# Feed-forward activations of an encoder trunk turned by block turns on VectorE and a trip through device memory instead of transposes on TensorE

## The chip, the cores and the metric

The kernel runs on one core of one Trainium2 chip. The metric is device time in microseconds for one launch. The kernel before was run three times: 1505.3, 1506.34 and 1506.68 us, median 1506.34 us.

## The reference, cut to what matters

Two layers over 512 tokens of width 1024, all in float32. Each layer adds a token mixer (windowed attention in layer 0, gated linear attention in layer 1) and then a feed-forward part:

```
def swiglu(h, w_gate_up, w_down):
    g, u = jnp.split(h @ w_gate_up, 2, axis=-1)
    return (jax.nn.silu(g) * u) @ w_down
...
for i in range(DEPTH):
    ...
    h = h + swiglu(rms_norm(h, ffn_norm[i]), ffn_w_gate_up[i], ffn_w_down[i])
```

`w_gate_up` is 1024 x 5632 (2816 gate and 2816 up columns), `w_down` is 2816 x 1024. The change touches only this part, which runs twice.

## The kernel before, in words

**Layout.** The residual `h` is kept with its 1024 features on partitions (8 tiles of 128 x 512 tokens). Every float32 operand of a large product is split into a high part (a copy on ScalarE, line 96) and a low part (a subtraction on VectorE, line 97), and a product is three matmuls: high by high, high by low, low by high.

**Gate and up** (`gate_up`, line 332). The 2816 hidden columns go in six chunks `j`: five of width 512 and a last one of width 256. The gate/up product of a chunk is done by a scheme with seven block products in place of eight (calls of `product`, lines 317 to 330; 24 matmuls each, results in PSUM banks `pp` and `s`). Here the activations are the stationary operand, so a chunk's result has tokens on partitions: `h1` (tokens 0 to 255) and `h2` (tokens 256 to 511), each 128 partitions x 2 x width, in buffers `g`. ScalarE copies results out of PSUM (line 367), VectorE combines and scales them (lines 381, 409, 410, 419, 431), ScalarE applies SiLU (lines 382, 429). `h1` is complete about when the sixth product runs, `h2` shortly after the seventh ends.

**Weights of a chunk** (`forms`, line 237). Each product needs a sum of blocks of the weight matrix. The sums are made by loads on SyncE's queue (SP, line 246, into `wA`, `wB`, `wf`) and accumulating loads on GpSimd's queue (line 251), and one by VectorE (line 296). The loads of a chunk are issued a chunk ahead; the accumulating loads can start only when the block before was split out of the same buffer. Split tiles `wh` and `wl` have three buffers each, so a split waits until the product three tiles back is through.

**The turn** (`turn`, line 348). The down product needs the activations with hidden columns on partitions. So 22 tiles `acts` of 128 x 512 are made, four per chunk of 512 columns. Before, each is four TensorE transposes of 128 x 128 (line 353) into a PSUM bank `t` or `o`, and one copy by ScalarE (line 355). The four turns of chunk `j` stand between the first five products of chunk `j+1`; the two of the last chunk stand among the first matmuls of the down product.

**Down** (`halves`, `down_part`, `down`, lines 441 to 477). Each of the 22 tiles is split into high and low parts (lines 446, 447). Then for each of the 8 output tiles `m`, 22 x 3 matmuls accumulate in a `pp` bank (`mm3`, lines 108 to 110), and VectorE adds the result to the old `h`, which was parked in device memory (`kept`) and is loaded again (line 473; the add is line 475). Down weights are loaded in three pieces per `m` into two buffers `wf` (line 103) and split. The first two tiles of the down product are started while the last chunk still runs.

**Order.** A scheduler with priorities and explicit "issue after" hints puts the instructions on each engine; each engine, and each DMA queue, then takes its own list strictly in order. An instruction that waits holds everything behind it on the same engine or queue.

Of the kernel before, what the change touches and what calls it, by code (L numbers as in the profile page):

```python
# [13 lines left out]
F32 = mybir.dt.float32  # L14
F32R = mybir.dt.float32r
AF = mybir.ActivationFunctionType
# [5 lines left out]
P = 128  # L22
D = 1024
S = 512
KT = D // P
NT = S // P
# [3 lines left out]
NH = HID // P  # L30
# [9 lines left out]
class Trunk:  # L40
# [291 lines left out]
    def gate_up(self, layer, acts):  # L332
        nc = self.nc
        ACT, DVE = nc.scalar.activation, nc.vector
        weights = [self.forms(self.ins["gate_up"][layer, j], j == 0, 0 if j else 2 * AHEAD) for j in range(5)]
        weights.append(self.forms(self.ins["gate_up_last"][layer], True))
        self.minus = self.t("Rc", (P, 256))
        first = next(weights[0])
        DVE.tensor_scalar(self.minus[:, 0:4], self.cols[:, self.col0 + 4:self.col0 + 8], -1.0, None, op0=ALU.mult)
        S1, S2, S3, S4 = [[(hi[:, i], lo[:, i]) for f, hi, lo in self.sums] for i in range(4)]  # L340
        self.kept = self.dr.tile([KT, P, S], F32, name=f"h_dram_{layer}")
        cut = lambda lo: [tuple(e[:, lo:lo + 256] for e in self.x[m]) for m in range(KT // 2, KT)]
        A11, A12, A22 = self.x[0:KT // 2], cut(0), cut(256)

        done = None
        late = [self.t("xs") for _ in range(NH - KT)]

        def turn(c):
            if done is None:
                return  # L350
            pt = self.p("to"[c % 2])
            for i in range(NT):
                nc.tensor.transpose(pt[:, i * P:(i + 1) * P], done[i // 2][:, i % 2, c * P:(c + 1) * P], self.ident)
            a = self.t("h") if len(acts) < KT else late[len(acts) - KT]
            ACT(a, pt, AF.Copy)
            acts.append(a)

        for j in range(6):
            width = 512 if j < 5 else 256
            w = weights[j]  # L360
            pair = lambda tag: [self.p(tag) for _ in range(2)]
            keep = lambda: self.t("g", (P, 2, S))

            def copy(src):
                out = keep()
# [11 lines left out]
            turn(1)  # L377
            def gates():
                for i in range(2):
                    e = g1[:, i, 0:width]  # L380
                    DVE.tensor_add(e, b2[i][:, 0:width], e)
                    ACT(e, e, AF.Silu, scale=R[:, i:i + 1])

            if j > 0:
                gates()
            b3 = pair("s")
            x5 = next(w)
            if j == 0:
                with self.tc.issue_after(self.low.ins):
                    self.last_sums()  # L390
            self.product(b3, S1, x5, width, True)
            turn(2)
# [7 lines left out]
            turn(3)  # L400
# [12 lines left out]
            if j == 4:  # L413
                before = self.copied
                with self.tc.high_priority(offset=AHEAD), self.tc.issue_after(before.ins):
                    early = [self.split(a, (P, S), tag, tag) for a, tag in zip(acts, ("a", "xs"))]
            for i in range(2):
                e = h2[:, i, 0:width]
                DVE.tensor_add(e, p5[:, i, 0:width], e)
            x4 = next(w)  # L420
            if j == 0:
                with self.tc.issue_after(self.added.ins):
                    for m in range(KT):
                        nc.gpsimd.dma_start(self.kept[m], self.h[m])
            self.product(b1, A22, x4, width, False)
            g2 = keep()
            for i in range(2):
                e = g2[:, i, 0:width]
                silu = ACT(e, b1[i][:, 0:width], AF.Silu, scale=R[:, 2 + i:3 + i])
                u = h2[:, i, 0:width]  # L430
                DVE.scalar_tensor_tensor(u, u, R[:, 6 + i:7 + i], e, op0=ALU.mult, op1=ALU.mult)
# [3 lines left out]
        self.started = self.down_part(self.p("pp"), layer, 0, 0, 2, early)  # L435
        for c in range(2):
            turn(c)
        with self.tc.issue_after(silu.ins):
            nc.scalar.preload_act_table_set("natural_log_exp_and_others")

# [21 lines left out]
    def down(self, layer, acts, col_next):  # L462
        nc = self.nc
        ps, pairs = self.started
        for k in range(len(pairs), NH):
            pairs.append(self.halves(acts[k], k))
        self.x = [None] * KT
        for m in range(KT):
            if m > 0:
                ps = self.p("pp")  # L470
            self.down_part(ps, layer, m, 2 if m == 0 else 0, NH, pairs)
            h = self.t("h")
            nc.sync.dma_start(h, self.kept[m])
# [751 lines left out]
```

## Time and profile before

| what | value |
|---|---|
| median of three runs | 1506.34 us |
| the profiled execution | 1506.73 us |
| its span, first to last instruction | 1504.9 us |
| first feed-forward part: chunks 1 to 4 | 628.6 to 789.7 us, about 40.2 us each |
| chunk 5 and the start of the down product | 789.7 to 829.5 us |
| second feed-forward part: transposes seen from, to | 1198.8 to 1382.8 us |
| granted TensorE clock | 1.000 |

Times are in us from the span's start unless marked ns. PE is TensorE, PEld its weight loads, DVE VectorE, ACT ScalarE, POOL GpSimd, SP SyncE, which issues DMAs. A row of a group says how often an instruction ran, its busy time and the mean of one. Matmuls overlap: each takes about 390 ns from start to end, but the next starts 227 ns later, so steps between starts, not durations, tell what TensorE spends.

### The profile page before, as it was taken

The page shows a single profiled execution, that of the slowest core. Times are in us where ns is not written, and L with a number is a line of the kernel's source. Part 1 is how long each engine was busy: PE and PEld are TensorE (multiplying, and loading weights), DVE is VectorE, ACT ScalarE, POOL GpSimd, SP SyncE. Part 2 cuts the span into 40 slices and gives each one's busy share as a digit, 9 for nine tenths or more (in the row PEclk, how much of TensorE's full clock was granted, in tenths as well). Part 3 has the DMA queues.
Part 4 walks back from the last instruction along what each step waited for, and adds up shares of the span by engine and source line. Part 5 has one row for each costly group of instructions (what it writes and reads, how often), then busy time and mean ns, then how long its engine had stood idle before and what let it go on. Part 6 is the DMA issues. An engine that isn't in the chain of part 4 may idle for free.

```text
span 1504.9 us, 21152 instructions
## 1 busy us (share of the span) xinstructions
PE 1490.5 (99%) x8142; PEld 1226.2 (81%) x8142; DVE 950.4 (63%) x1732; ACT 784.9 (52%) x1352; POOL 110.2 (7%) x192
## 2 busy tenths in 40 slices
PE   8999999999999999999999999999999999999998
PEld 6878788877878878888889887888888888889887
DVE  6584666768477778866667334947576866668222
ACT  6353453545366655755567323546644855568121
POOL 0001010101010011211110000000010211110000
PEclk9999999999999999999999999999999999999999
DMA  7412222243222137776664333212155676675331
GB/s 277 163 60 93 85 82 84 79 125 99 84 71 71 43 111 204 224 166 146 151 152 135 104 91 104 88 57 84 47 160 185 196 172 152 156 151 147 121 107 60
DMA packets 59829, 183.95 MB, mean 122 GB/s; under 512 B 10032, under 2 KB 10608, under 8 KB 59728
## 3 DMA queue, kind: packets, MB, share of 16 engines
q1 hardware_dynamic: 44912, 133.17, 26.6%
q0 software_dynamic: 14816, 49.42, 16.2%
q8 instruction: 64, 1.05, 0.3%
q14 instruction: 37, 0.30, 0.1%
HBM read 174.11 MB, written 8.46 MB: 121 GB/s over the span
## 4 chain that ended last, share of the span: by engine, by line
PE 87%; DVE 8%; ACT 2%; DMA 1%; issue 1%; SPq 0%; ACTq 0%; DVEq 0%
PE ppp L109 9%; PE ppp L108 9%; PE ppp L110 9%; PE ppp L548 7%; PE ppp L549 7%; PE ppp L547 7%; PE ppp L328 6%; PE ppp L330 6%; PE ppp L329 6%; PE ps L330 3%; PE ps L328 3%; PE ps L329 3%; PE po L679 2%; DVE wl L97 2%; PE ps L639 1%; PE ps L729 1%
## 5 line engine op out<-in xcount | busy, mean ns | idle before, releaser
L97 DVE TENSOR_TENSOR wl<-wf,wh 128x1024 fp32r<-128x1024 f32 (+1 forms) x184 | 220.3, 1199 | 229.2 <-ACT wh L96 228.5
L96 ACT ACTIVATE wh<-wf 128x1024 fp32r<-128x1024 f32 (+1 forms) x184 | 191.4, 1041 | 319.9 <-PE ppp L109 192.7
L547 PE MATMUL ppp<-wh,xs 128*128 128x512 f32 (+1 forms) x672 | 256.9, 386 | 5.8 <-ACT wh L96 5.5
L548 PE MATMUL ppp<-wl,xs 128*128 128x512 f32 (+1 forms) x672 | 257.8, 384 | 0.6 <-DVE wl L97 0.3
L549 PE MATMUL ppp<-wh,xs 128*128 128x512 f32 (+1 forms) x672 | 257.6, 383 | 0.0
L547 PEld LDWEIGHTS ppp<-wh,xs 128*128 128x128 f32 x672 | 126.8, 189 | 33.1 <-ACT wh L96 5.5
L548 PEld LDWEIGHTS ppp<-wl,xs 128*128 128x128 f32 x672 | 126.8, 189 | 26.4 <-DVE wl L97 2.7
L549 PEld LDWEIGHTS ppp<-wh,xs 128*128 128x128 f32 x672 | 126.9, 189 | 25.0 <-issue 1.3
L97 DVE TENSOR_TENSOR wl<-wA,wh 128x1024 fp32r<-128x1024 f32 x88 | 107.4, 1221 | 37.9 <-ACT wh L96 37.9
L96 ACT ACTIVATE wh<-wA 128x1024 fp32r<-128x1024 f32 x88 | 93.2, 1059 | 62.0 <-PE ppp L330 45.8
L328 PE MATMUL ppp<-wh,a 128*128 128x512 f32 (+1 forms) x288 | 108.2, 381 | 0.0
L329 PE MATMUL ppp<-wl,a 128*128 128x512 f32 (+1 forms) x288 | 107.4, 373 | 0.0
L330 PE MATMUL ppp<-wh,a 128*128 128x512 f32 (+1 forms) x288 | 107.3, 374 | 0.0
L109 PE MATMUL ppp<-xs,wh 128*128 128x512 f32 x272 | 106.6, 393 | 0.0
L108 PE MATMUL ppp<-xs,wh 128*128 128x512 f32 x272 | 106.3, 392 | 0.0
L110 PE MATMUL ppp<-xs,wl 128*128 128x512 f32 x272 | 105.9, 391 | 0.0
L97 DVE TENSOR_TENSOR wl<-wB,wh 128x1024 fp32r<-128x1024 f32 x38 | 46.5, 1225 | 73.7 <-ACT wh L96 73.7
L627 ACT ACTIVATE sm<-sm,st 128x160 f32<-128x160 f32 (+2 forms) x128 | 56.8, 447 | 40.8 <-DVE st L626 40.7
L328 PE MATMUL ps<-wh,sh 128*128 128x512 f32 (+1 forms) x192 | 73.1, 381 | 0.0
L328 PE MATMUL ppp<-wh,sh 128*128 128x512 f32 (+1 forms) x192 | 72.2, 376 | 0.0
L330 PE MATMUL ppp<-wh,sl 128*128 128x512 f32 (+1 forms) x192 | 71.6, 373 | 0.0
L330 PE MATMUL ps<-wh,sl 128*128 128x512 f32 (+1 forms) x192 | 71.5, 373 | 0.0
(323 smaller groups left out, 2957.3 us busy)
## 6 DMA issues: line engine op xcount, KB each, us to landing
wA<-in_gate_up_dram POOLq DMA_DIRECT2D x52, 512.0 KB, 5.4
wf<-in_down_dram SPq DMA_DIRECT2D x32, 512.0 KB, 3.6
wf<-in_gate_up_dram SPq DMA_DIRECT2D x24, 512.0 KB, 4.5
wf<-in_a_w_v_dram SPq DMA_DIRECT2D x20, 512.0 KB, 3.4
wB<-in_gate_up_dram POOLq DMA_DIRECT2D x20, 512.0 KB, 5.5
wf<-in_a_w_q_dram SPq DMA_DIRECT2D x16, 512.0 KB, 3.3
wf<-in_a_w_qk_dram SPq DMA_DIRECT2D x16, 512.0 KB, 3.2
wB<-in_gate_up_dram SPq DMA_DIRECT2D x16, 512.0 KB, 3.2
```

Source lines behind the costliest of these rows:

```text
L96: nc.scalar.activation(hi, src, AF.Copy)
L97: self.low = nc.vector.tensor_sub(lo, src, hi.bitcast(F32))
L108: mm(out, lhsT=wh, rhs=xh, start=start, stop=False)
L109: mm(out, lhsT=wh, rhs=xl, start=False, stop=False)
L110: self.multiplied = mm(out, lhsT=wl, rhs=xh, start=False, stop=stop)
L328: mm(a, lhsT=xh[:, tok], rhs=wh[:, f], start=start and k == 0, stop=False, skip_group_check=True)
L329: mm(a, lhsT=xh[:, tok], rhs=wl[:, f], start=False, stop=False, skip_group_check=True)
L330: self.multiplied = mm(a, lhsT=xl[:, tok], rhs=wh[:, f], start=False, stop=k == last, skip_group_check=True)
L547: mm(a, lhsT=xh, rhs=wh[:, f], start=k == 0, stop=False)
L548: mm(a, lhsT=xh, rhs=wl[:, f], start=False, stop=False)
L549: self.multiplied = mm(a, lhsT=xl, rhs=wh[:, f], start=False, stop=k == KT - 1)
L627: nc.scalar.activation(sm[:, w], sm[:, w], AF.Exp, bias=n, scale=-1.0, accum_out=l)
```

## The change

It replaces the way in which the finished activations get hidden columns on partitions; the arithmetic stays the same.

- `turn` is now on VectorE: one instruction turns a 128 x 512 piece in blocks of 32 x 32 (line 351 of the kernel after). For each 256 hidden columns of a chunk there is a buffer `y` of 128 x 1024, with room in the pool `g`, filled half from `h1` and half from `h2`. That is four block turns per full chunk, two in the last: 22 per layer, 44 in all.
- `put` stores each `y` to device memory (`turned`) by four DMAs on SP's queue (line 359), one for each group of 32 partitions, in runs of 128 numbers (512 bytes). These four put the 32 x 32 blocks where a full transpose would have them, apart from the order of tokens.
- `get` loads one finished tile of 128 x 512 back (line 365), on SP's queue, at the places where a turn stood before. A fetch waits for the four stores of its `y`.
- The tokens of the turned tiles come in another order (within 512: 4 groups of 32 out of each 128). The down product's result has that order too, and the add to `h` (line 489, before 475) reads and writes with a pattern that undoes it.
- TensorE's 176 transposes and ScalarE's 44 copies out of PSUM are gone.

```
-        def turn(c):
-            if done is None:
-                return
-            pt = self.p("to"[c % 2])
-            for i in range(NT):
-                nc.tensor.transpose(pt[:, i * P:(i + 1) * P], done[i // 2][:, i % 2, c * P:(c + 1) * P], self.ident)
-            a = self.t("h") if len(acts) < KT else late[len(acts) - KT]
-            ACT(a, pt, AF.Copy)
-            acts.append(a)
+        turned = self.dr.tile([NH, 4, 32, 4, P], F32, name=f"turned_{layer}")
+
+        def turn(half, done, ys):
+            for n, y in enumerate(ys):
+                f = slice(n * 256, (n + 1) * 256)
+                DVE.transpose(y.rearrange("p b g j -> p g b j")[:, 2 * half:2 * half + 2],
+                              done[:, :, f].rearrange("p i (b j) -> p i b j", j=32))
+
+        def put(ys):
+            for n, y in enumerate(ys):
+                c = 4 * j + 2 * n
+                to = turned[c:c + 2].rearrange("c b i a e -> a i (c b) e")
+                for r in range(4):
+                    nc.sync.dma_start(to[r], y[32 * r:32 * r + 32].rearrange("i b g j -> i b (g j)"))
+
+        def get():
+            c = len(acts)
+            if c < min(4 * j, NH):
+                a = self.t("h") if c < KT else late[c - KT]
+                nc.sync.dma_start(a, turned[c].rearrange("b i a e -> (b i) (a e)"))
+                acts.append(a)
...
-            with self.tc.issue_after(self.multiplied.ins):
-                turn(0)
+            get()
...
+            ys = [self.t("g", (P, 8, 4, 32)) for _ in range(width // 256)]
+            turn(0, h1, ys)
             self.product(b1, S3, next(w), width, False)
...
-            done = (h1, h2)
+            turn(1, h2, ys)
+            put(ys)
...
-            nc.vector.tensor_add(h, ps, h)
+            order = "p (g a j) -> p a g j"
+            nc.vector.tensor_add(h.rearrange(order, a=4, j=32), ps.rearrange("p (a g j) -> p a g j", a=4, j=32),
+                                 h.rearrange(order, a=4, j=32))
```

Line numbers after the diff are larger by 10 to 15 in the kernel after (418, 419, 430, 442, 460 and 489 there are 409, 410, 419, 431, 447 and 475 before).

Three places show what stands where now.

First, SP's queue in the first feed-forward part, about the end of chunk 1. Before, it holds only weight loads (`wA` and one `wf` for chunk 3, then `wf` and `wB` for chunk 3):

```order
L246 DMA wA_7033<-in_gate_up_dram 128x1024
L246 DMA wA_7035<-in_gate_up_dram 128x1024
L246 DMA wf_7080<-in_gate_up_dram 128x1024
L246 DMA wf_7082<-in_gate_up_dram 128x1024
L246 DMA wB_7130<-in_gate_up_dram 128x1024
```

After, the eight stores of chunk 1 (two buffers `g`, four DMAs each) and its four fetches (into `h`) stand between them:

```order
L246 DMA wA_7036<-in_gate_up_dram 128x1024
L246 DMA wA_7038<-in_gate_up_dram 128x1024
L246 DMA wf_7078<-in_gate_up_dram 128x1024
L359 DMA turned_6095<-g_6645 32x8x128 x4
L359 DMA turned_6095<-g_6646 32x8x128 x4
L365 DMA h_6773<-turned_6095 128x512
L365 DMA h_6816<-turned_6095 128x512
L246 DMA wf_7080<-in_gate_up_dram 128x1024
L365 DMA h_6862<-turned_6095 128x512
L365 DMA h_6901<-turned_6095 128x512
L246 DMA wB_7123<-in_gate_up_dram 128x1024
```

The second `wf` load of chunk 3 and its `wB` loads now stand behind stores that wait for the end of chunk 1, and behind fetches that wait for these stores.

Second, VectorE where chunk 4 goes over into chunk 5 in the first feed-forward part. `wl` are weight splits, `a`, `xs` and `wA` from `h` are halves of finished tiles. Before:

```order
L97 TENSOR_TENSOR wl_7609<-wA_7336,wh_7608 128x1024
L419 TENSOR_TENSOR g_7591<-g_7473,g_7591 128x512
L97 TENSOR_TENSOR wl_7646<-wf_7643,wh_7645 128x1024
L97 TENSOR_TENSOR a_7595<-h_6464,a_7594 128x512
L97 TENSOR_TENSOR xs_7599<-h_6512,xs_7598 128x512
L419 TENSOR_TENSOR g_7591<-g_7473,g_7591 128x512
L447 TENSOR_TENSOR wA_7908<-h_6563,wA_7908 128x512
L447 TENSOR_TENSOR wA_7911<-h_6607,wA_7911 128x512
L97 TENSOR_TENSOR wl_7695<-wf_7692,wh_7694 128x1024
```

After:

```order
L351 STREAM_TRANSPOSE g_7534<-g_7493 128x2x8x32
L97 TENSOR_TENSOR wl_7590<-wA_7333,wh_7589 128x1024
L351 STREAM_TRANSPOSE g_7535<-g_7493 128x2x8x32
L430 TENSOR_TENSOR g_7572<-g_7455,g_7572 128x512
L97 TENSOR_TENSOR wl_7637<-wf_7634,wh_7636 128x1024
L97 TENSOR_TENSOR a_7576<-h_6474,a_7575 128x512
L97 TENSOR_TENSOR xs_7580<-h_6517,xs_7579 128x512
L430 TENSOR_TENSOR g_7572<-g_7455,g_7572 128x512
L460 TENSOR_TENSOR wA_7886<-h_6563,wA_7886 128x512
L460 TENSOR_TENSOR wA_7889<-h_6602,wA_7889 128x512
L97 TENSOR_TENSOR wl_7681<-wf_7678,wh_7680 128x1024
```

Two block turns of `h1` have come in ahead of the split (the last row of each piece) that the second product of chunk 5 waits for.

Third, SP's queue at the start of the down product. Before, the weight pieces follow one another (last of `m` = 0, the three of `m` = 1, the first of `m` = 2):

```order
L103 DMA wf_8042<-in_down_dram 128x768
L103 DMA wf_8076<-in_down_dram 128x1024
L103 DMA wf_8106<-in_down_dram 128x1024
L103 DMA wf_8136<-in_down_dram 128x768
L103 DMA wf_8171<-in_down_dram 128x1024
```

After, the stores of the last chunk and its two fetches (`xs`) stand among them:

```order
L103 DMA wf_8010<-in_down_dram 128x768
L365 DMA xs_6091<-turned_6095 128x512
L365 DMA xs_6092<-turned_6095 128x512
L103 DMA wf_8044<-in_down_dram 128x1024
L486 DMA h_8413<-h_dram_6080 128x512
L486 DMA h_8508<-h_dram_6080 128x512
L359 DMA turned_6095<-g_7813 32x8x128 x4
L103 DMA wf_8074<-in_down_dram 128x1024
L103 DMA wf_8104<-in_down_dram 128x768
L365 DMA xs_6093<-turned_6095 128x512
L365 DMA xs_6094<-turned_6095 128x512
```

The last two fetches, of tiles 20 and 21, stand behind the third weight piece of `m` = 1.

More of the change, by code (lines that the diff above doesn't have):

```diff
@@ L343, in gate_up @@
         A11, A12, A22 = self.x[0:KT // 2], cut(0), cut(256)
-        done = None
         late = [self.t("xs") for _ in range(NH - KT)]
-        def turn(c):
-            if done is None:
-                return
-            pt = self.p("to"[c % 2])
-            for i in range(NT):
-                nc.tensor.transpose(pt[:, i * P:(i + 1) * P], done[i // 2][:, i % 2, c * P:(c + 1) * P], self.ident)
-            a = self.t("h") if len(acts) < KT else late[len(acts) - KT]
-            ACT(a, pt, AF.Copy)
-            acts.append(a)
+        turned = self.dr.tile([NH, 4, 32, 4, P], F32, name=f"turned_{layer}")
[16 more added lines that the diff above has]
+                acts.append(a)
         for j in range(6):
@@ L376, in gate_up @@
             self.product(b2, A12, next(w), width, True)
-            turn(1)
+            get()
             def gates():
@@ L391, in gate_up @@
             self.product(b3, S1, x5, width, True)
-            turn(2)
+            get()
             p5 = copy(b3)
@@ L399, in gate_up @@
             self.product(b1, S2, x6, width, False)
-            turn(3)
+            get()
             if j == 0:
@@ L435, in gate_up @@
         self.started = self.down_part(self.p("pp"), layer, 0, 0, 2, early)
+        j = 6
         for c in range(2):
-            turn(c)
+            get()
         with self.tc.issue_after(silu.ins):
```

## The prediction

> **What bounds the kernel now.** I read the page first, then the busy time by stretches, then TensorE instruction by instruction, then the chain of waits. The page's first part gives the engines:
>
> ```profile
> PE 1490.5 (99%) x8142; PEld 1226.2 (81%) x8142; DVE 950.4 (63%) x1732; ACT 784.9 (52%) x1352; POOL 110.2 (7%) x192
> ```
>
> TensorE looks full, but a busy TensorE may only be one whose matmuls overlap. So the stretches of chunks 2 and 3 and the end of the first feed-forward part (length, then busy time and instructions of PE, PEld, DVE, ACT, POOL, then clock, DMA share, GB/s):
>
> ```profile
> 669.10:709.30 40.20, 40.20 (x185) 32.99 (x184) 25.47 (x27) 23.49 (x31) 5.15 (x6) 1.00 0.69 159
> 709.30:749.50 40.20, 40.20 (x185) 32.98 (x184) 25.48 (x27) 23.51 (x31) 5.16 (x6) 1.00 0.67 155
> 789.70:812.90 23.20, 22.77 (x187) 22.19 (x187) 19.29 (x27) 18.95 (x34) 0.86 (x1) 1.00 0.55 161
> ```
>
> Two chunks take 40.20 us each with the same instruction count, at full clock, while VectorE has some 15 us free in each and ScalarE 17. That is a steady issue rate, not a wait. TensorE's rows in time show the rate (start, duration):
>
> ```profile
> 639.45 0.39 PE L328 MATMUL ppp<-wh,a 128*128 128x512 f32 x1
> 639.68 0.39 PE L329 MATMUL ppp<-wl,a 128*128 128x512 f32 x1
> 639.90 0.39 PE L330 MATMUL ppp<-wh,a 128*128 128x512 f32 x1
> 640.14 0.60 PE L353 MATMUL po<-ident,g 128*128 128x128 f32 x4
> 640.49 0.48 PE L328 MATMUL ps<-wh,sh 128*128 128x512 f32 x1
> 640.80 0.40 PE L329 MATMUL ps<-wl,sh 128*128 128x512 f32 x1
> ```
>
> The step from matmul to matmul is 0.227 us. Across a turn, 639.90 to 640.80 is 0.90 us for two steps, which would be 0.45: a turn of four transposes costs the stream 0.45 us. TensorE bounds the chunks, and the transposes are in its stream.
>
> **What is removed.** The rows of the transposes, both PSUM banks:
>
> ```profile
> L353 PE MATMUL po<-ident,g 128*128 128x128 f32 x88 | 14.9, 272 | 0.0
> L353 PE MATMUL pt<-ident,g 128*128 128x128 f32 x88 | 14.5, 274 | 1.0 <-DVE g L431 1.0
> ```
>
> 176 transposes are 44 turns. At 0.45 us each that is 19.8 us. The chunks say a little more: 40.20 less 7 x 24 = 168 matmuls at 0.227 (38.14) is 2.06 us for four turns, because the scheduler cuts one turn of each chunk in two and the stream is disturbed twice (0.7 for that one). Eight chunks (1 to 4, two layers) give 16.5 us; the remaining 12 turns (four beside chunk 5 and two in the down product, per layer) at 0.45 give 5.4. In chunk 5 TensorE also waits for a turn's input:
>
> ```profile
> 792.88 0.36 PE L328 MATMUL ppp<-wh,a 128*128 128x256 f32 x1
> 793.09 0.28 PE L329 MATMUL ppp<-wl,a 128*128 128x256 f32 x1
> 793.80 0.33 PE L353 MATMUL pt<-ident,g 128*128 128x128 f32 x1 [0.43 <-DVE g L431]
> ```
>
> The wait of 0.43 goes too, once a layer: 0.9. Gross gain 16.5 + 5.4 + 0.9 = 22.8 us. ScalarE's 44 copies (line 355) count nothing: ScalarE is not late in the chunks.
>
> The Trainium skill would size this otherwise: "VectorE: DVE Perf Modes", section "The three transpose paths", gives 390 ns for a TensorE transpose of 128 x 128 (bf16) and 311 ns for VectorE's 32 x 32 blocks, and the section "Rules for kernel authors" prefers TensorE for a full 128 x 128. By its figure 176 transposes would be an estimated 68.6 us. The trace does not agree for transposes within a stream: 0.45 us for four is 0.11 each, so less is to be won.
>
> **What is added on VectorE.** 44 block turns of 128 x 512. Before has block turns of 32 columns only; for 512 columns it has other operations:
>
> ```profile
> L667 DVE STREAM_TRANSPOSE t<-sm 128x32 f32<-128x32 f32 x64 | 9.4, 188 | 7.7 <-ACT sm L627 7.4
> L419 DVE TENSOR_TENSOR g<-g,g 128x512 f32<-128x512 f32 x4 | 2.7, 682 | 0.0
> ```
>
> If a block turn runs one column per cycle like the addition, it takes 0.68 us, of which 0.60 count back to back; if each 32 columns paid the 0.19 of the small one, 16 x 0.19 = 3.0. I take 0.68: most of 0.19 us for 32 columns must be fixed cost. Four in a chunk are 2.7 us against 15 free. They stand in line, though: two before the weight splits of the next chunk. In chunks 1 to 4 each split is ready about a microsecond or more before its matmul, so I cost them at nothing there; uncovered they would be 0.6 us each.
>
> Where chunk 4 goes into chunk 5 that cover is gone. The chain of waits runs there through DMA, ScalarE and VectorE and not through TensorE:
>
> ```profile
> 772.75 5.44 DMA wB<-in_gate_up_dram
> ...
> 788.87 1.18 DVE wA L447 x2
> 790.04 0.03 issue
> 790.07 1.02 DVE wl L97
> ...
> 793.08 0.67 DVE g L431
> ```
>
> The split at 790.07, whole length 1.21, ends at 791.28 and now comes behind two block turns: 792.5. Its matmul ran at 793.09; without the turns since that load (a whole one, 0.45, and most of a cut one, 0.6) it would run at 792.0. TensorE waits about 0.5 us, once a layer: 1.0.
>
> The final add reads and writes in groups of 32 numbers, 16 times. Only the last add of the program lies on the path, so I cost it at nothing; bounds 0 and one more pass over it, 0.7 us.
>
> **What is added on the queues.** Per full chunk: eight stores of 128 KB, four fetches of 256 KB. The nearest rows (KB each, median us to landing) and the cost of issuing on SP:
>
> ```profile
> out_dram<-h SPq DMA_DIRECT2D x8, 256.0 KB, 2.0
> h<-h_dram SPq DMA_DIRECT2D x8, 256.0 KB, 3.2
> h_dram<-h POOLq DMA_DIRECT2D x8, 256.0 KB, 7.5
> L1215 SPq DMA_DIRECT2D out_dram<-h x8: 343/344/344, 1396.5 to 1501.2; - x8
> ```
>
> Twelve issues at 0.34 are 4 us of SP per chunk, plus the wait of the fetches for the stores. What waits behind is the next-but-one chunk's `wf` and `wB`: loaded a chunk ahead, they have some 20 us to spare, so this is hidden. The DMA engines get 2 MB more per chunk; the store goes in 512-byte runs. A short stretch that held only 128 such packets and 16 tiny ones, and the queues of chunk 2:
>
> ```profile
> q1 hardware_dynamic: 144, 0.07, 32.2%
> DMA  8999997920000004999799999596492294475849
> q0 software_dynamic: 875, 3.19, 45.4%
> q1 hardware_dynamic: 864, 3.15, 22.8%
> ```
>
> 32.2% of 0.7 us on 16 engines for 128 packets is 28 ns each; 2048 per chunk are 3.6 us of all engines. The fetch, at q1's 9.2 us for 3.15 MB, is 3.1 us. So the share of 0.69 rises to about 0.86 of a shorter chunk; the slices of 1 us show eight empty ones just where the fetches fall. Hidden, with less to spare.
>
> **The down product's start** has least cover. Tiles 20 and 21 go turn, store, fetch, halves. In before's times: VectorE's last line-431 operation ends at 815.5, the turn at 816.2, stores issued by 817.6 and landed by 819.6. The fetches then stand behind the third weight piece of `m` = 1, the last of these four issues:
>
> ```profile
> 809.24 12.61 SPq L103 DMA_DIRECT2D wf<-in_down_dram  x4
> 820.14 1.14 ACT L446 ACTIVATE g<-xs 128x512 fp32r<-128x512 f32 x2
> 826.94 0.39 PE L108 MATMUL ppp<-g,wh 128*128 128x512 f32 x1
> ```
>
> The issues end at 821.85 (809.24 + 12.61), so the fetches issue at 822, land at 825.2 and 825.5, and the halves, made by ScalarE from 820.14 before, are ready by about 826.6 and 827.3. TensorE wanted tile 20 at 826.94 and, two turns earlier, wants it at 826.0: a wait of about 0.5 us a layer, 1.0.
>
> **The sum**, against the profiled execution's own 1506.73 us (span 1504.9 and 1.8 around it): 1506.7 - 22.8 + 1.0 + 1.0 = 1485.9. The median of the runs lies 0.4 below the profiled one: **1485.5 us**. If only 0.45 per turn goes, 1488.5; if neither wait comes, 1483.5.
>
> **The rivals.**
>
> A. The fetches come later still. A store that lands like `h_dram` (7.5 in place of 2.0) lands at 825.1, the halves are ready near 830, and TensorE waits 3.5 us more a layer: 1485.5 + 7 = 1492.5. For it: that row is a store beside accumulating loads. Against: the down product's start has no accumulating load of its own chunk left. Chance 0.13.
>
> B. VectorE sets the end in the chunk change. At 1.4 us a block turn, the two ahead of the split add 1.5 us, the two behind the next sum another 0.7, and the second split of each chunk's seventh product, with 0.6 to spare, is late by 0.1 eight times: about 2 x 2.2 + 0.8 = 5 us, 1490.5. At 3.0 us a turn, some 15 us. For it: the chain already runs through VectorE there. Against: the fixed cost seen at 32 columns. Chance 0.12.
>
> C. Slower: stores crowd the accumulating loads. The second load for a chunk's third product issues at
>
> ```profile
> 669.43 0.85 POOL L251 DMA_DIRECT2D wA<-in_gate_up_dram  x1 [1.95 <-DVE wl L97]
> DMA to landing us min/median/max: 5.2/5.4/10.7
> ```
>
> Its tile is wanted at 669.1 + 60 x 0.227 + 0.9 = 683.6, less 2.3 for the split: 681.3. Stores start at about 674. With a landing at the slowest seen, 680.1, nothing happens. If the stores hold it 13.5 us beyond a usual landing of 674.9, to 688.4, TensorE waits 7 us in each of eight chunks: 1485.5 + 56 = 1541.5. It decides from a delay of 6.4 us, where a wait begins; above 9.0 us (2.6 x 8 = 20.8, all that the sum gains) the change is slower. Against: the stores' own engine time is 3.6 us. "VectorE: DVE Perf Modes", section "The three transpose paths", of the Trainium skill warns that a plain DMA copy that transposes by strides is 19 times slower than one through the crossbar when the innermost stride is large. By that rule C would be the likely case; here the innermost 128 numbers are in one run, and the 28 ns packet speaks against it. Chance 0.08.
>
> D. The same crowding between these points eats the gain to within 0.2% (3 us, about what a measurement of this kernel can tell from no change). Chance 0.04.
>
> **How the numbers follow.** The forecast keeps 0.63, its own range 1483.5 to 1488.5. Faster by over 0.2%: forecast, A and B, 0.88; same 0.04; slower 0.08. The range takes in A, B's nearer half and, below, a microsecond for splits that gain more: 1482.5 to 1495, leaving out C, D and a part of B.
>
> **What would show it.** Chunks of about 38.1 us with 168 matmuls and steps of 0.227 would show the gain; longer steps at a chunk's third or sixth product, released by a DMA, rival C. Line 351's mean is the block turn. A gap before the matmul of chunk 5's second product, and one before tile 20, of about half a microsecond each, are the two costs. Chunks still near 40 us, or a gap of several us in each, would make the prediction wrong.

## The result, and the profile after

The changed kernel takes 1528.64 us (median of four runs, 1525.56 to 1530.77) against 1506.13 before (four runs): 1.0147 times as long, 95% interval 1.0135 to 1.0159. The prediction was 1485.5 us and faster with a chance of 0.88. It was wrong in sign: 43.1 us lie between forecast and result.

The page of the kernel after, its engines, its DMA totals, its chain and the queue of the accumulating loads (KB each, median us to landing):

```profile
PE 1485.6 (97%) x7966; PEld 1212.6 (80%) x7966; DVE 976.5 (64%) x1776; ACT 765.3 (50%) x1308; POOL 110.2 (7%) x192
...
DMA packets 90103, 207.02 MB, mean 136 GB/s; under 512 B 12145, under 2 KB 35249, under 8 KB 90001
...
PE 67%; issue 18%; DVE 7%; DMA 3%; ACT 3%; POOL 2%; POOLq 0%; SPq 0%; ACTq 0%; DVEq 0%
...
L351 DVE STREAM_TRANSPOSE g<-g 128x512 f32<-128x512 f32 x44 | 30.2, 701 | 0.6
...
wB<-in_gate_up_dram POOLq DMA_DIRECT2D x20, 512.0 KB, 7.2
```

TensorE has lost its 176 transposes and 5 us of busy time, and yet idles 38 us (1523.8 less 1485.6) where it idled 14. The block turn takes 0.70 us, as forecast. The last row is the first hint: before, it read

```profile
wB<-in_gate_up_dram POOLq DMA_DIRECT2D x20, 512.0 KB, 5.5
```

Laid beside each other, matmul by matmul, the two kernels keep a steady distance up to the first feed-forward part (after is 1.3 us ahead there) and again between the two parts. All of the loss falls inside them: 9.9 us in layer 0 and 10.4 in layer 1. By part, both layers together, the two traces differ by 11.8 us in chunk 0, 5.4 in chunks 1 to 4, and 3.1 in chunk 5 and the 66 matmuls of the first down output. Chunks 0 to 5 of layer 0, after, in the busy time by stretches (columns as in the prediction):

```profile
588.05:632.72 44.67, 41.47 (x177) 33.03 (x176) 38.41 (x58) 29.84 (x43) 7.80 (x12) 0.96 0.61 183
632.72:676.68 43.96, 40.62 (x170) 32.45 (x168) 27.67 (x30) 22.03 (x27) 4.25 (x5) 0.96 0.72 179
676.68:717.14 40.46, 38.98 (x170) 31.30 (x168) 27.03 (x31) 21.67 (x27) 4.87 (x6) 1.00 0.81 206
717.14:756.65 39.51, 38.84 (x169) 31.23 (x168) 27.40 (x31) 21.88 (x27) 4.94 (x7) 1.00 0.87 213
756.65:796.51 39.86, 39.05 (x169) 31.24 (x168) 27.60 (x31) 24.39 (x32) 6.57 (x8) 1.00 0.83 198
796.51:823.78 27.27, 23.54 (x177) 21.68 (x176) 23.43 (x34) 17.24 (x31) 0.86 (x1) 1.00 0.72 196
```

Before, chunks 0 and 1 took 39.2 and 40.6 and chunk 5 took 23.1; they now take 44.7, 44.0 and 27.3. Chunks 2 to 4 hardly gain: 39.5 to 40.5 where 38.1 was forecast. Within a chunk the loss has one place. Lengths of the seven products of chunk 2, layer 0, from the starts of TensorE's rows (two later runs, explained below, beside them). A length runs to the first matmul of the next product, so a wait for the sixth product's first weight split counts in the fifth:

| kernel | 1 to 4 | 5 | 6 | 7 |
|---|---|---|---|---|
| before | 5.80, 5.81, 5.91, 5.91 | 5.55 | 5.61 | 5.62 |
| after | 5.44, 5.44, 5.44, 5.44 | 6.32 | 6.77 | 5.61 |
| without transposes (`bare2`) | 5.44, 5.44, 5.44, 5.44 | 5.44 | 6.18 | 5.90 |
| the same without the accumulating load of the sixth (`bare_noadd`) | 5.44, 5.44, 5.44, 5.44 | 5.44 | 5.61 | 5.58 |

The first four products have become 24 x 0.227 us, just as forecast; what they win is given back while TensorE waits for the weight splits of the sixth. Who TensorE waits for, in the stretch of chunks 0 to 5, before and then after:

```profile
PE pt L353 <- DVE g L431: 0.4, 1, 0.4
```

```profile
PE ppp L328 <- ACT wh L96: 5.6, 4, 2.6
PE ppp L329 <- DVE wl L97: 4.3, 7, 0.8
PE ppp L328 <- ACT g L377: 2.3, 2, 2.0
PE ps L328 <- ACT g L377: 0.7, 1, 0.7
```

Weight splits come late now, and in chunk 5 copies out of PSUM (line 377). Two things stand out, and they are told apart below.

**At the end of chunk 0 TensorE's order has turned over.** At 622.92 it waits for a split, when no store has been issued yet:

```profile
622.92 0.88 PE L328 MATMUL ppp<-wh,a 128*128 128x512 f32 x2 [1.15 <-ACT wh L96]
624.18 0.80 PE L329 MATMUL ppp<-wl,a 128*128 128x512 f32 x1 [0.38 <-DVE wl L97]
```

The list of TensorE in the built program says why. Before, the seventh product follows the sixth (`ppp_6095` and `ppp_6096` are chunk 0's banks); after, most of the first product of chunk 1 (banks `ppp_6436`, `ppp_6437`) comes in between:

```
before  L330 MATMUL ppp_6096<-wh_6343,sl_6048 128x512
before  L328 MATMUL ppp_6095<-wh_6376,a_5872 128x512
after   L330 MATMUL ppp_6097<-wh_6348,sl_6048 128x512
after   L328 MATMUL ppp_6436<-wh_6442,a_5890 128x512
```

`wh_6442` has to wait for one of the three split buffers, while the seventh product's splits lie ready. Steps over 0.4 us from 622 to 631 add up to 5.3 us of loss.

**In the later chunks an accumulating load lands late.** The four of chunk 1 in the view of line 251 (issues, then the time to landing), before and after:

```profile
L251 POOL DMA_DIRECT2D wB<-in_gate_up_dram x2: 850/850/850, 648.9 to 652.1; - x2
...
DMA to landing us min/median/max: 5.3/5.4/5.5
```

```profile
L251 POOL DMA_DIRECT2D wB<-in_gate_up_dram x2: 850/850/850, 651.9 to 654.6; - x2
...
DMA to landing us min/median/max: 8.9/9.4/9.6
```

and TensorE at the sixth product of chunk 1, after, with 3.3 us of idle time:

```profile
659.70 0.39 PE L330 MATMUL ps<-wh,sl 128*128 128x512 f32 x1
662.66 0.51 PE L328 MATMUL ppp<-wh,sh 128*128 128x512 f32 x1 [2.58 <-ACT wh L96]
663.92 0.50 PE L329 MATMUL ppp<-wl,sh 128*128 128x512 f32 x1 [0.76 <-DVE wl L97]
```

Chunk 5 waits for a late accumulating load too, by way of ScalarE's queue. Its own load took 7.1 us to landing where it took 5.3 before, and the split that needs it stands ahead of the two copies that TensorE waits for, 2.0 us, at 814.91:

```profile
813.53 1.06 ACT L96 ACTIVATE wh<-wA 128x1024 fp32r<-128x1024 f32 x1 [2.50 <-DMA wA<-in_gate_up_last_dram]
```

### The profile page after: what moved, and what is told of

It reads as the page before. It is cut to its first block, busy times and chain, and to the rows that moved or that the text cites. A ratio compares the mean times of both kernels' runs of the same rounds, so it can differ in the third digit from the quotient of the medians.

```text
span 1523.8 us, 21053 instructions
## 1 busy us (share of the span) xinstructions
PE 1485.6 (97%) x7966; PEld 1212.6 (80%) x7966; DVE 976.5 (64%) x1776; ACT 765.3 (50%) x1308; POOL 110.2 (7%) x192
## 4 chain that ended last, share of the span: by engine, by line
PE 67%; issue 18%; DVE 7%; DMA 3%; ACT 3%; POOL 2%; POOLq 0%; SPq 0%; ACTq 0%; DVEq 0%
PE ppp L110 9%; PE ppp L109 9%; PE ppp L108 9%; PE ppp L563 8%; PE ppp L564 8%; PE ppp L562 8%; PE po L694 2%; PE ppp L328 2%; PE ppp L329 2%; PE ppp L330 2%; PE ps L654 1%; POOL wA L251 1%; DVE wl L97 1%; DMA wB<-in_gate_up_dram 1%; PE ps L744 1%
## 5 line engine op out<-in xcount | busy, mean ns | idle before, releaser
L329 PE MATMUL ppp<-wl,sh 128*128 128x512 f32 (+1 forms) x192 | 74.7, 389 | 5.0 <-DVE wl L97 4.8
```

What stands on the lines that cost most here:

```text
L329: mm(a, lhsT=xh[:, tok], rhs=wl[:, f], start=False, stop=False, skip_group_check=True)
```

## The experiments

Twelve kernels were run, each timed beside the kernel before on the same chip (medians of before there: 1506.67, 1506.24 and 1506.91 us). The ratios are the recorded estimates; they differ by up to 0.0008 from the quotients of the medians.

| run | median us | ratio to before, 95% interval |
|---|---|---|
| `late` | 1517.22 | 1.0062 (1.0045 to 1.0079) |
| `local` | 1516.17 | 1.0063 (1.0048 to 1.0078) |
| `late_local` | 1503.22 | 0.9975 (0.9966 to 0.9984) |
| `late_stores` | 1506.24 | 0.9996 (0.9987 to 1.0005) |
| `late_fetch` | 1511.27 | 1.0035 (1.0022 to 1.0048) |
| `bare` | 1509.05 | 1.0017 (1.0006 to 1.0028) |
| `bare2` | 1497.20 | 0.9938 (0.9923 to 0.9952) |
| `bare_noadd` | 1487.94 | 0.9876 (0.9861 to 0.9890) |
| `before_turns` | 1509.04 | 1.0018 (1.0008 to 1.0027) |
| `late_local_loop` | 1491.93 | 0.9905 (0.9888 to 0.9921) |
| `late_loop` | 1491.23 | 0.9899 (0.9884 to 0.9914) |
| `late_fetch_loop` | 1490.34 | 0.9894 (0.9880 to 0.9909) |

### Order or transfers: `late`, `local`, `late_local`, `late_stores`

The first theory was that the inversion and the transfers make the loss. The copy of the sixth product, `h2`, takes a buffer of the pool `g`. The change takes the two `y` buffers from the same pool one line earlier, and their first writer needs the token norm, which is ready late in chunk 0. If the pool serves its requests in program order, the copy is held until then, and with it the seventh product, which adds to the bank that is to be copied. So one run moves that line:

```
-            ys = [self.t("g", (P, 8, 4, 32)) for _ in range(width // 256)]
-            turn(0, h1, ys)
             self.product(b1, S3, next(w), width, False)
             h2 = copy(b1)
+            ys = [self.t("g", (P, 8, 4, 32)) for _ in range(width // 256)]
+            turn(0, h1, ys)
```

> The changed kernel with one move: the two tiles for the block turns are taken from the pool g after the copy of h2 and no longer ahead of it; all transfers stay. TensorE's order then has chunk 0's seventh product ahead of chunk 1's first again, as before the change. Theory (order): chunks 0 and 1 together, 88.6 and 88.2 us in the two layers after the change, fall to some 80 or less, since the inversion alone opened 5.3 us of gaps from 622 to 631 us and delayed the transfers that then met the accumulating loads; all in all 16 to 20 us less than the 1528.6 of the changed kernel, 1508 to 1512. Rival (transfers): the accumulating loads are late by the stores and fetches whatever the order; only the 5 us of gaps per layer go, 1517 to 1519. Rival (VectorE): the block turns themselves are the cost; 1525 or more.

Measured: 1517.22, 11.4 less than the changed kernel. TensorE's list has the old order again and chunk 0 is back at 39.2 us. That is the rival's number, not the theory's: the inversion cost what chunk 0 had grown by, 5.5 and 6.4 us in the two layers, and no more. Chunk 1 stays long:

```profile
588.83:628.07 39.24, 39.24 (x178) 32.27 (x176) 35.36 (x54) 28.24 (x41) 6.92 (x11) 1.00 0.63 197
628.07:670.95 42.88, 39.62 (x170) 31.16 (x168) 29.54 (x35) 23.27 (x30) 5.11 (x6) 1.00 0.77 192
```

The transfers were taken out with the order as it is, and with the order mended (`put` copies on ScalarE, `get` does nothing; `late_stores` keeps the stores beside these copies):

```
-                for r in range(4):
-                    nc.sync.dma_start(to[r], y[32 * r:32 * r + 32].rearrange("i b g j -> i b (g j)"))
+                for k in range(2):
+                    ...
+                    ACT(a, y.rearrange("p b g j -> p (b g j)")[:, k * S:(k + 1) * S], AF.Copy)
```

> The changed kernel, its inverted order in chunk 0 kept, without stores and fetches: ScalarE copies each block-turned tile to the activation tile (as many copies as before the change had), so the 32-row bands are not exchanged and the numbers stand in other places. Theory (order and transfers): the 10 to 11 us of chunks 0 and 1 that the order costs per layer shrink to the 5 us of the gaps, the accumulating loads land in 5.5 us again, and chunks 2 to 4 take 38.2 each: 1497 to 1502. Rival (order alone): the transfers cost nothing, 1525 to 1529. Rival (VectorE): 1515 or more, with the gaps at the sixth product still there.

> Both: tiles taken after the copy of h2, and no stores or fetches (ScalarE copies instead; bands not exchanged). What is left of the change is the transposes that TensorE no longer does and the 44 block turns on VectorE. Theory (order and transfers are the loss): near the sum of the prediction, chunks 1 to 4 at 38.2 to 38.5 us, all in all 1486 to 1492, chunk 5 alone longer than its 21 us. Rival (VectorE's turns are a third of the loss or more): 1497 or more.

> Tiles taken after the copy of h2, the eight stores per chunk kept, no fetches (ScalarE copies instead; bands not exchanged). Theory (the traffic as such, 2 MB of stores with 512-byte packets and 1 MB of fetches): about two thirds of the way from the run without transfers to the run with both. Rival (small packets of the stores): as slow as with both, within 2 us. Rival (the fetches stand in SP's queue or crowd the loads): as fast as without transfers, within 2 us.

Measured: 1516.17, 1503.22 and 1506.24. Order and transfers add up: either alone mended gives 11.4 and 12.5, both give 25.4. Of the 14.0 us from `late` to `late_local` the stores make 3.0 and the fetches 11.0, though the stores move the same 1 MB per chunk in four times the packets (the expectation gave them 2 MB, which was a slip). The last rival of `late_stores` comes nearest. The rows of `late` in chunk 1 show why, first POOL's and SP's issues, then how long the loads and the fetches took to land:

```profile
642.72 0.85 POOL L251 DMA_DIRECT2D wA<-in_gate_up_dram  x1 [13.24 <-DVE wl L97]
645.05 0.85 POOL L251 DMA_DIRECT2D wA<-in_gate_up_dram  x1 [1.48 <-DVE wl L97]
...
638.48 4.26 SPq L359 DMA_DIRECT2D turned<-g  x8
642.92 2.88 SPq L365 DMA_DIRECT2D h<-turned  x4
```

```profile
wA<-in_gate_up_dram POOLq DMA_DIRECT2D x2, 512.0 KB, 8.5
h<-turned SPq DMA_DIRECT2D x4, 256.0 KB, 9.4
wB<-in_gate_up_dram POOLq DMA_DIRECT2D x2, 512.0 KB, 9.3
turned<-g SPq DMA_DIRECT2D x5, 128.0 KB, 2.5
```

The fetches start in the same microseconds as the accumulating loads, and both are slow. Without the fetches the four loads took 5.9 to 6.6 us. Chunk 1 is the worst case: in chunk 2 of `late` the fetches land in 2.9 to 4.3 us, the last of them 3.4 us after the first accumulating load was issued, and the four loads take 6.2 to 7.9 us. But the theory's numbers for `local` and `late_local` were missed by 14 and 11 us: with no transfer and the right order 17.7 us to the forecast are still missing, and the waits at the sixth product are still there. There is a third part, and the rival's VectorE was the next to ask.

### What is still missing: `bare`, `bare2`, `bare_noadd`, `before_turns`

`before_turns` adds the 44 block turns to the kernel before and lets nobody read them (`blocks` is the changed kernel's `turn`):

```
             h2 = copy(b1)
+            ys = [self.t("g", (P, 8, 4, 32)) for _ in range(width // 256)]
+            blocks(0, h1, ys)
...
             done = (h1, h2)
+            blocks(1, h2, ys)
```

> The kernel before with all its transposes, and the 44 block turns added on VectorE, their tiles taken from the pool g after the copy of h2 and read by nobody. It prices the turns alone. Prediction: nothing in chunks 1 to 4, about a microsecond per layer at most around chunk 5: 1506 to 1508. Theory (VectorE is part of the loss): chunk 5 longer by 2 to 4 us per layer, since its chain runs through VectorE: 1510 to 1515.

Measured: 1509.04, 2.8 us more than before, between the two. TensorE's wait in chunk 5 of layer 0 grows from 0.43 to

```profile
794.53 0.33 PE L353 MATMUL pt<-ident,g 128*128 128x128 f32 x1 [1.42 <-DVE g L439]
```

In the traces about 1 us of it falls in chunk 5 of each layer and 1 in chunk 1 of layer 1. So VectorE is a cost, but a small one. Then the gross gain alone: the kernel before, the transposes left out.

```
-            for i in range(NT):
-                nc.tensor.transpose(pt[:, i * P:(i + 1) * P], done[i // 2][:, i % 2, c * P:(c + 1) * P], self.ident)
-            ACT(a, pt, AF.Copy)
+            ACT(a.rearrange("p (i f) -> p i f", i=2), done[c % 2][:, :, lo:lo + 256], AF.Copy)
```

> The kernel before, with TensorE's transposes left out: ScalarE copies the same number of untransposed activations to the activation tiles, so that these hold other numbers. No block turns, no transfers. It measures the gross gain alone. Prediction's sum: 22.8 us less than the 1506.1 of before, 1483.3, chunks 1 to 4 at 38.1. Theory (loop): with the transposes gone, the 48 matmuls from the release of a split buffer to the second tile of a chunk's sixth product are 10.9 us, as long as the splits and the accumulating load that must fit there (10.8 in the run without transfers), so each chunk keeps a wait of half a microsecond or more: 1486 to 1491, chunks at 38.6 to 39.0.

> As the run without transposes (bare), but ScalarE copies from the second of the two activation tiles of a chunk alone: there, copies of the first tile stood ahead of the copies of the sixth product on ScalarE and made TensorE wait 2.3 us more in six of eight chunks, which was this test's own doing. Again no transposes, no block turns, no transfers, other numbers in the activation tiles. Prediction's sum: 1483.3. Theory (loop): chunks 1 to 4 at 38.9 to 39.3 with the wait at the sixth product, and the seventh's 5.6 and 23.5 in chunk 5: 1493 to 1500.

`bare` gave 1509.05, far from either expectation, because copies of `h1` stood in ScalarE's way (TensorE waits 5.9 us for ScalarE's copies in chunks 1 to 4 of layer 0); `bare2` (`done[1]` in place of `done[c % 2]`) is the clean run: 1497.20. Leaving out all 176 transposes, with nothing in their place on any other queue, wins 9.7 us and not 22.8. `bare_noadd` (the line `add("wB", 2)` gone) shows what holds the rest back:

> The same without transposes, and the accumulating load of a chunk's sixth product left out (its tile is used without that block added). Theory (loop): the waits at the sixth product vanish, chunks 1 to 4 at 38.2, 1482 to 1485. Rival: what is missing to 1483.3 in the run with the load is not that load; no change from it.

Measured: 1487.94, with every chunk 1 to 4 of layer 0 at 38.39 us. It was made from `bare`, but products of 5.4 to 5.6 us show that `bare`'s own fault did not come through; against `bare2` it is 9.3 us less. That is 3 us above the theory's range: chunks 1 to 4 behave as the theory said, and chunk 5 stays at 23.15 us. The rows of the first tile of chunk 2's sixth product, before, from the issue of its accumulating load to its matmul with the low part:

```profile
689.15 0.86 POOL L251 DMA_DIRECT2D wB<-in_gate_up_dram  x1 [1.87 <-DVE wl L97]
...
694.53 1.06 ACT L96 ACTIVATE wh<-wB 128x1024 fp32r<-128x1024 f32 x1 [2.22 <-DMA wB<-in_gate_up_dram]
695.62 1.23 DVE L97 TENSOR_TENSOR wl<-wB,wh 128x1024 fp32r<-128x1024 f32 x1 [3.59 <-ACT wh L96]
698.33 0.39 PE L329 MATMUL ppp<-wl,sh 128*128 128x512 f32 x1
```

and in `bare2`:

```profile
687.45 0.86 POOL L251 DMA_DIRECT2D wB<-in_gate_up_dram  x1 [1.86 <-DVE wl L97]
...
693.76 1.06 ACT L96 ACTIVATE wh<-wB 128x1024 fp32r<-128x1024 f32 x1 [2.93 <-DMA wB<-in_gate_up_dram]
694.86 1.22 DVE L97 TENSOR_TENSOR wl<-wB,wh 128x1024 fp32r<-128x1024 f32 x1 [4.98 <-ACT wh L96]
696.13 0.50 PE L329 MATMUL ppp<-wl,sh 128*128 128x512 f32 x1 [0.28 <-DVE wl L97]
```

Before, the low part is ready at 696.85 and wanted at 698.33: 1.5 us to spare. In `bare2` it is ready at 696.08 and TensorE has been waiting. The load may go only when the same buffer has been split for the fifth product, that split waits for one of three split buffers, and TensorE frees them at its own pace: it is a loop through POOL, DMA, ScalarE and VectorE beside TensorE's stream, nearly as long as that stream was. In `bare2` chunks 1 to 4 take 38.7 to 40.1 us with it, in `bare_noadd` 38.4 to 38.7 without that load. Take the transposes away and the stream gets shorter and the loop longer: the loads follow each other more closely, and from issue to split it is 6.3 us in place of 5.4.

### Moving the fetches: `late_fetch`

SP's fetches were put behind weight loads (`self.loaded` is the newest load of `forms`). In layer 0 those of chunks 0 and 1 were issued at the end of the following chunk, at 665.8 and 706.6 us, and those of chunks 2 and 3 together at 790.0, at the end of chunk 4:

```
+            if j > 2:
+                with self.tc.issue_after(self.loaded.ins):
+                    for c in range(4):
+                        get(j - 3)
...
             self.product(b1, A11, w1, width, True)
-            get()
```

> The changed kernel with the tiles taken after the copy of h2 and the same stores and fetches, but the four fetches of a chunk's tiles are issued on SP after the weight loads at the end of the following chunk and not while its accumulating loads run; all numbers as in the reference. Theory (the fetches cost because they meet the accumulating loads): accumulating loads land in 6 us or so and the time comes within 3 us of the 1506.2 without fetches: 1505 to 1509. Rival (the traffic costs wherever it is): as with the fetches in place, 1515 to 1518.

Measured: 1511.27, in the middle. Six of the eleven microseconds of the fetches go with their place; the rest stays. In their new place they meet other accumulating loads: the one issued at 670.3 us took 10.0 us to landing.

### Giving the loop room: `late_local_loop`, `late_loop`, `late_fetch_loop`

If a loop of loads and splits sets the pace, one product more between the two uses of `wB` should free it. The change had made room for that: its two PSUM banks `t` and `o` are no longer used by transposes, so in chunks 1 to 4 the product with `S4` can have its own banks and stand ahead of the one with `S2` (`own` is true for chunks 0 and 5, which keep the old order):

```
-            if not own: add("wB", 2)
+            if not own:
+                add("wB", 2)
+                add("wA", 1)
...
-        for step in (first, second, fifth, sixth, third, seventh, fourth):
+        for step in (first, second, fifth, *((sixth, third) if own else (third, sixth)), seventh, fourth):
...
+            if not own:
+                b3 = [self.p(tag) for tag in "to"]
+                self.product(b3, S4, next(w), width, True)
             x6 = next(w)
...
                 DVE.tensor_add(e, b3[i][:, 0:width], e)
+                if not own:
+                    DVE.tensor_add(e, p5[:, i, 0:width], e)
```

> Block turns on VectorE, tiles taken after the copy of h2, no stores or fetches (ScalarE copies; bands not exchanged), and in chunks 1 to 4 the product with S4 stands ahead of the one with S2, in the two PSUM banks that the transposes had. The accumulating load for the sixth product then has one product more to land in. Theory (loop): chunks 1 to 4 at 38.2 to 38.5, and of the 1503.2 with the old order of products the waits at the sixth product go: 1490 to 1496. Rival (the load is late for the DMA engines' sake, or VectorE sets the pace): 1500 or more.

> The changed kernel with the tiles taken after the copy of h2 and, in chunks 1 to 4, the product with S4 ahead of the one with S2 as in the run beside it; all stores and fetches where the change puts them; all numbers as in the reference. Theory (loop): 5.4 us more of slack take in landings of 8 to 9 us as well, so from 1517.2 the waits of chunks 1 to 4 go and those of chunk 5 stay: 1495 to 1502. Rival (the transfers fill the DMA engines): 1508 or more.

> Candidate: tiles taken after the copy of h2, fetches a chunk later behind the weight loads, and in chunks 1 to 4 the product with S4 ahead of the one with S2; all numbers as in the reference. Theory (loop and fetches both): from 1511.3 chunks 1 to 4 fall from 40.8 on average to 38.5, 18 us less: 1491 to 1497, faster than both kernels. Rival: the loop only moves to the tile of the seventh product, whose second load is now behind the sixth's; 1503 or more.

Measured: 1491.93, 1491.23 and 1490.34, as the theory said or, in `late_loop`, 4 us below its range. Chunks 1 to 4 and 5 of layer 0 in `late_loop`, which has every transfer of the change where the change puts it:

```profile
628.36:667.55 39.19, 39.03 (x169) 31.24 (x168) 31.58 (x37) 23.34 (x30) 5.13 (x6) 1.00 0.88 215
667.55:706.26 38.71, 38.69 (x169) 31.38 (x168) 29.43 (x33) 21.67 (x27) 5.15 (x6) 1.00 0.89 218
706.26:744.96 38.70, 38.68 (x169) 31.38 (x168) 29.42 (x33) 21.67 (x27) 5.16 (x6) 1.00 0.88 217
744.96:783.66 38.70, 38.68 (x169) 31.38 (x168) 29.77 (x34) 24.15 (x32) 6.07 (x7) 1.00 0.93 214
783.66:805.49 21.83, 21.14 (x171) 20.53 (x170) 19.68 (x29) 16.03 (x29) 0.86 (x1) 1.00 0.66 173
```

TensorE has no gap left in chunks 2 to 4, at a DMA share of 0.88 to 0.93. Yet the accumulating loads of chunk 1 are nearly as slow here as in `late` (8.2, 9.0 and 9.3 there):

```profile
DMA to landing us min/median/max: 8.2/8.3/8.7
```

So the transfers are not cheap in themselves; with 5.4 us more before anyone needs the load they cost nothing that can be measured (1491.2 with, 1491.9 without). The two PSUM banks alone could also have helped, but in chunks 1 to 4 of layer 0 of `late_local` TensorE waited for low parts of weight splits only (0.9 us in three waits), and in `late_local_loop` for nothing. Not all of the gain lies there, though. Between the traces of `late_local` and `late_local_loop` 3.7 us fall in chunks 1 to 4 and 5.2 in chunk 5 and the first down output, whose products keep their order; between `late` and `late_loop` it is 21.4 and 6.9. How the move helps chunk 5 was not traced. With the move, `late_loop` is 1.0% faster than the kernel before and 2.4% faster than the changed one (1491.23 to 1528.64). Moving the fetches as well adds no clear gain. In the kernel before the new order of products was not tried: its transposes need the two banks, and its TensorE has no gap in a chunk to win.

## Why the prediction was wrong, step by step

**"TensorE bounds the chunks"** was true, but not the whole of it. The price of a turn in the stream, 0.45 us, was right: products one to four fell to 5.44 us. The step that failed is the one that followed: "In chunks 1 to 4 each split is ready about a microsecond or more before its matmul, so I cost them at nothing there". The prediction weighed that slack against the block turns alone and not against its own gain of 2 us per chunk; at the sixth product of chunk 2 it was 1.5 us. The transposes were cover for a loop that needs nearly the whole chunk. Gross gain: 22.8 forecast, 9.7 measured (`bare2`). By part, in the traces: in chunks 1 to 4 16.5 were booked, `bare2` gained 8.5, and `bare_noadd` 15.0. In chunk 5 and the first down output 6.3 were booked (5.4 and 0.9), `bare2` gained 2.3 and `bare_noadd` 4.2: there the transposes covered other waits, in `bare2` for the low part of a weight split (0.6 us) and for one of ScalarE's copies (0.5 us).

A smaller step was mis-sized as well. The 2.06 us per chunk were put down to the turns alone, but without any transpose `bare_noadd` still takes 38.39 us and not 38.14: the sixth and seventh product take 5.6 us before as after, and no transpose stands among them.

**"Hidden, with less to spare"**, of the DMA engines, failed in the same place. The share of 0.69, or 0.86 after, is a mean over a chunk (0.86 is the new work over the old chunk of 40.2 us; over the forecast 38.1 it would be 0.90, and `late_loop` shows 0.88 to 0.93). In stretches of 2 us the kernel before shows what it is made of:

```profile
683.00:685.00 2.00, 2.00 (x11) 1.65 (x10) 0.84 (x3) 1.20 (x2) 0.86 (x1) 1.00 0.00 0
685.00:687.00 2.00, 2.00 (x13) 1.67 (x12) 1.12 (x1) 1.55 (x3) 0.58 (x1) 1.00 1.06 176
...
695.00:697.00 2.00, 2.00 (x11) 1.65 (x10) 1.23 (x1) 1.56 (x3) 0.00 (x0) 1.00 0.99 199
```

Empty for 6 us (679 to 685), then full for 12, while the four accumulating loads run. The prediction saw the empty slices (six of 1 us, which it counted as eight), but the fetches wait for the stores: in chunk 1 of `late` they start just when the empty stretch ends, and in chunk 2 they fill it and run over by 3.4 us. This is close to rival C, at a smaller size (up to 4 us of delay and not 13.5) and with another culprit: C named the stores, which cost 3.0 us, and the fetches cost 11.0. The rival was priced at the third product, which has 6.4 us of room; the sixth, with 1.5, was named only under what would show it. Cost: 14.0 us with the order mended. The Trainium skill, "DMA: Bandwidth & Descriptors", section "Queues, rings and completion order", says that an engine takes its queues in turn, a packet at a time. The trace agrees as far as it goes: loads and fetches that overlap both slow down, to medians of 8.5 to 9.4 us in chunk 1 of `late`; the order of their packets was not looked at.

**The inversion** appears in no step. The prediction looked at the lists of SP and VectorE, and not at TensorE's, where removing instructions seemed to need no look. It cost 11.4 us.

**What held:** the block turn (0.70 us, forecast 0.68), the wait before chunk 5's second product (0.41 us at 800.07, forecast 0.5), the final add (0.69 us before and after), and SP's queue (no split in chunks 1 to 4 of layer 0 waits for a load into `wf`). Rival A's late fetches did not come, and neither did the half microsecond that the prediction itself gave tile 20: in layer 0 TensorE has no wait from 824 to 860 us, nor in `late_loop` from 805 to 860. The block turns as a whole cost 2.8 us beside the transposes (`before_turns`) where 1.0 was allowed.

**The account.** Of the 43.1 us between forecast and result, 11.4 are the order (`late`), 14.0 the transfers (to `late_local`), 11.3 the new order of products (to `late_local_loop`), 6.4 are left. In the traces that last step is only in part the loop of chunks 1 to 4, as shown above. Of what is left, about half is chunks of 38.7 in place of 38.1, whose fifth to seventh product take 5.6 to 5.7 us and not 5.44, and half is the chunk 1 of each layer, with 39.1 and 40.6. What disturbs the stream there was not traced. These are differences of medians of kernels whose runs spread over some 5 us (`late` 1514.55 to 1519.23, `late_local` 1500.41 to 1507.05), so each step is good to 2 or 3 us. Transfers and loop are one cause seen twice: with the loop given room the transfers cost nothing, and without it both are paid.

## What to carry to other kernels

Before you book a gain on the busiest engine, find the second-longest chain of the same stage and its slack, load by load; the gain ends there, and anything added to a resource of that chain can cost at once. Read a resource's share in stretches as short as the waits that matter, not as a mean over the stage. And compare the instruction lists of every engine, also of those that only lose work: a buffer taken from a shared pool one line earlier was enough to turn over TensorE's order.

## What the runs showed of the hardware

TensorE's clock fell to half after short idle stretches, so that some waits were paid twice. After the wait of chunk 1 (kernel after):

```profile
664.00:665.00 1.00, 1.00 (x3) 0.83 (x4) 0.00 (x0) 0.94 (x1) 0.00 (x0) 0.65 0.09 33
665.00:666.00 1.00, 1.00 (x4) 0.75 (x3) 0.85 (x1) 1.00 (x2) 0.00 (x0) 0.50 0.93 311
666.00:667.00 1.00, 1.00 (x4) 0.81 (x3) 1.00 (x3) 0.06 (x1) 0.00 (x0) 0.50 0.46 180
```

Matmuls stepped by 0.43 us there for about 3 us, which adds some 1.6 us to idle stretches of 2.58 and 0.76. Idle stretches of 0.72 and 0.75 us in chunk 2, and one of 1.96 in chunk 5, left the clock at 1.00. The Trainium skill, "TensorE: Matmul & The Clock Gate", section "Part 1: The HAM clock gate", gives the half clock after an idle window of some 3.4 us. Around 662 us the trace comes near that: 3.3 us of idle time, with one matmul in between. It does not agree at 623 us. There the clock was halved for some 3.4 us (0.67 in the slice from 623, 0.50 in the next two, 0.62 in the one from 626), when the only idle stretch shortly before was one of 1.15 us. Another of 1.15 us, six microseconds later, left it at 1.00:

```profile
628.00:629.00 1.00, 0.00 (x0) 0.00 (x0) 0.00 (x0) 1.00 (x2) 0.00 (x0) 1.00 1.07 213
```

So the length of one wait does not decide it. Eight matmuls of one column each stood just ahead of the first of these two waits; whether they count as nearly idle time, no run here shows.
